# Two more quarters of each MLP's second matrix by seven block products, with the sums kept in DRAM

## The chip, the cores and the metric

The kernel runs on one core of one Trainium2 chip. The metric is the device time of one execution in microseconds (us); lower is better.

## The reference

A trunk of two layers on one sequence of 512 frames of width 1024, all in float32. Layer 0 has a gated linear recurrence (HGRN2), layer 1 a differential attention over keys and values projected once between the layers. Each mixer is followed by an output projection and an MLP, with an RMS norm ahead of and behind each part, and a residual sum:

```python
def squared_relu_mlp(h, w_up, w_down):
    u = jax.nn.relu(h @ w_up)
    return (u * u) @ w_down
...
    for layer in range(DEPTH):
        if layer < N_A:
            ...
            h = h + rms_norm(mix, a_norm_post[a])
        else:
            ...
            h = h + rms_norm(mix, b_norm_post[bi])
        ff = squared_relu_mlp(rms_norm(h, mlp_norm_pre[layer]), mlp_w_up[layer], mlp_w_down[layer])
        h = h + rms_norm(ff, mlp_norm_post[layer])
        if layer == N_A - 1:
            k_sh, v_sh = shared_kv(h, kv_norm, w_kv)
```

The MLP's inner width is 4096; here it is cut into four quarters of 1024. The change is in the two MLPs and in what they share buffers with.

## The kernel before

**Products.** Everything is kept transposed (features on the 128 partitions, frames along a row). A float32 product is made of three products of rounded halves: high by high, high by low, low by high (`mm3`, L114 for each matmul). The activations' halves are `xhi`, `xlo` (the MLP's input) and `uhi`, `ulo` (its inner values). Weights come by SP's DMA into a tile of tag "raw" (four buffers of 512 KB); ACT makes the high half `whi`, DVE the low half `wlo` (eight buffers each).

**Order.** `Plan` writes TensorE's order by hand; the instructions of the other engines stand in the order that the scheduler gave when the kernel was built. An engine takes its instructions, and each queue its transfers, in that fixed order, so a waiting instruction holds all that stands behind it. ACT's and DVE's queues hold splits of weights and evictions of PSUM one behind the other.

**The MLP (`block`).** Quarter 0 of the first matrix is dense (`up`, in two halves of the frames). Quarters 1 to 3 of it go by seven block products (`up_pair`): two row blocks of 128 outputs by two halves of 256 frames, as a 2 x 2 block matrix. One pair has seven products (PSUM names ux, uy, uz) of twelve matmuls of 256 columns, and there are four pairs p to a quarter. `sums_x` makes the sums of x's blocks once. The weights' sums are made per pair: raw_a holds the blocks a11 and a12; raw_s gets the block of row 3 twice by SP, and then the rows 0 and 1 are added to it by a DMA that GpSimd (POOL) issues with accumulate (L465); two sums of DVE (L473, L474) follow, in raw_a's place. raw_d holds the remaining block for two pairs. So two pairs take five raw tiles out of four buffers. The products' results are combined by ACT (p1, p5 and u2: copies out of PSUM, L486) and DVE (L496, L498, L500), then relu (L501, L502, L504), square (L409), uhi (L410), ulo (L411).

After each quarter's first matrix stands that quarter of the second matrix, dense: 192 matmuls of 512 columns (`dn`), whose sums DVE accumulates in the SBUF tile zacc (L538 the first time, L540 later). The last quarter is made by halves of the frames (`dn_h`, `dn_last`), so that the norm behind it (`bounds`) can start with the first half.

So TensorE's order in an MLP is: up, dn quarter 0, four pairs, dn quarter 1, four pairs, dn quarter 2, four pairs, dn quarter 3 by halves.

`params` (the attention's constants and the table bias_dr, written to DRAM by a POOL DMA of 1.25 MB) is spawned as a chain beside layer 0's output projection and MLP.

Of the kernel before, what the change touches and what calls it, by code (L numbers as in the profile page):

```python
# [17 lines left out]
P = 128  # L18
# [70 lines left out]
def trunk_kernel(ctx: ExitStack, tc: tile.TileContext, x_t, w_qf, w_g, w_i, w_ao, w_k, w_q, w_v, w_bo, w_up, w_us, w_dn,  # L89
# [44 lines left out]
    ones1 = cp.tile([P, P], F32, name="ones1")  # L134
    v.memset(ones1, 1.0)
# [25 lines left out]
    def split_w(raw, gain, pr, name):  # L161
# [3 lines left out]
        lo = wp.tile([P, per, ncols], F32R, tag="wlo", name=f"wlo_{name}_{pr}", bufs=8)  # L165
# [14 lines left out]
    def load_w(src, ncols, gain, name):  # L180
        out = []
        for pr in range(ncols // 128):
            out += split_w(fetch_w(src, ncols, pr, name), gain, pr, name)
        return out

# [71 lines left out]
    def bounds(pool, ps_list, zacc, h, gpost, eab, want, name, gpre=None):  # L257
# [92 lines left out]
        if want == "ea":  # L350

            a.activation(ea[:, lo:hi], ms, AF.Square, scale=math.sqrt(EPS), bias=eps15)
        else:
            s = rsqrt_rows((tmp[:, 3, 0], tmp[:, 3, 1]), ms, None)
            a.activation(rb[:, lo:hi], s, AF.Copy, scale=-0.5)
            yield W_RSTD
            pc = smt("ps_rc")
            for i in range(n // P):
                pe.matmul(pc[:, i:i + 1], rb[0:1, lo + i * P:lo + (i + 1) * P], ones1[0:1, 0:1], start=True, stop=True)
            v.tensor_copy(rcol[:, lo // P:hi // P], pc[:, :n // P])  # L360
# [26 lines left out]
    def out_proj(wsrc, gain, name, before_last):  # L387
        wt = [load_w(wsrc[i], 512, gain, f"{name}{i}") for i in range(2)]
        return by_halves(wt, uhi, ulo, name, before_last)

    def block(pool, proj, gpost, name, layer, want):

        gpre = gn[:, G_MPRE[layer]:G_MPRE[layer] + 8]
        zacc = pool.tile([P, 8, S], F32, name=f"zacc{layer}")
# [8 lines left out]
        def split_u(ps, pr, lo, hi, n):  # L403
            r = pool.tile([P, 2, S], F32, tag="r", name=n, bufs=2)[:, :, 0:hi - lo]
            a.activation(r, ps, AF.Relu)
            keep_u(r, pr, lo, hi)

        def keep_u(r, pr, lo, hi):
            a.activation(r, r, AF.Square)  # L409
# [31 lines left out]
        def split_b(raw, name):  # L441

            n = raw.shape[1]
            hi = wp.tile([P, 2, 512], F32R, tag="whi", name=f"whi_{name}", bufs=8)[:, 0:n, :]
            lo = wp.tile([P, 2, 512], F32R, tag="wlo", name=f"wlo_{name}", bufs=8)[:, 0:n, :]
# [4 lines left out]
        a22s = []  # L450

        def up_pair(q, p, ts):

            nm = f"{layer}_{q}_{p}"
# [3 lines left out]
            ws = w_us[layer, q - 1]  # L458
# [7 lines left out]
            if p % 2 == 0:  # L466
                rd = raw("d")
                nc.sync.dma_start(rd, ws[p:p + 2, :, 1, :].rearrange("a p f -> p a f"))
                a22s[:] = split_b(rd, f"d{nm}")
            a11, a12 = split_b(ra, f"a{nm}")  # L470
            a22 = a22s[p % 2]
# [4 lines left out]
            px, py, pz = mmt(f"ux{nm}")[:, 0:256], smt(f"uy{nm}")[:, 0:256], smt(f"uz{nm}")[:, 0:256]  # L476
            r = pool.tile([P, 2, S], F32, tag="r", name=f"r{nm}", bufs=2)
# [6 lines left out]
            def keep(ps, name):  # L484
                t = pool.tile([P, 256], F32, tag="ev", name=f"{name}{nm}", bufs=4)
# [3 lines left out]
            yield from prod(px, a11, xpart(0, 0), True)  # L489
            p1 = keep(px, "p1")  # L490
            yield from prod(pz, s1, ts[0], True)
            p5 = keep(pz, "p5")
            yield from prod(px, s2, ts[2], False)
            u2 = keep(px, "u2")
            yield from prod(py, a12, xpart(1, 0), True)
            v.tensor_tensor(r[:, 0, 0:256], py, p1, op=ALU.add)  # L496
            yield from prod(px, s3, ts[1], False)
            v.tensor_tensor(r[:, 1, 256:512], px, p5, op=ALU.add)  # L498
            yield from prod(pz, s4, xpart(1, 1), False)
            v.tensor_tensor(r[:, 0, 256:512], pz, u2, op=ALU.add)  # L500
            a.activation(r[:, 0, :], r[:, 0, :], AF.Relu)  # L501
            a.activation(r[:, 1, 256:512], r[:, 1, 256:512], AF.Relu, scale=-1.0)  # L502
            yield from prod(px, a22, ts[3], False)
            a.activation(r[:, 1, 0:256], px, AF.Relu, scale=-1.0)  # L504
            keep_u(r, p, 0, S)

        for q in range(4):
            if q == 0:
                wt = [load_w(w_up[layer, i], 512, None, f"up{layer}_{i}") for i in range(2)]
                for h, (lo, hi) in enumerate(halves):  # L510
                    yield until(("x", name, h))
                    for pr in range(4):
                        ps = mmt(f"up{layer}_{h}_{pr}").rearrange("p (j t) -> p j t", j=2)
                        for j in range(2):
                            n = 2 * pr + j
                            for kt in range(8):
                                wmm(ps[:, j, :], wt[n // 4], kt, (n % 4) * P, xhi, xlo, lo, hi, kt == 0, kt == 7)
                                yield 0
                        split_u(ps, pr, lo, hi, f"r{layer}_{h}_{pr}")
                ts = sums_x()  # L520
            else:
                for p in range(4):
                    yield from up_pair(q, p, ts)
            if q < 3:
                for i in range(2):
                    wt = load_w(w_dn[layer, q, i], 512, None, f"dn{layer}_{q}_{i}")
                    pss = [mmt(f"dn{layer}_{q}_{i}_{n4}") for n4 in range(4)]
                    if i == 0:
                        order = [(kt, n4) for kt in range(8) for n4 in range(4)]
                    else:  # L530
                        order = [(kt, n4) for n4 in range(4) for kt in range(8)]
                    for kt, n4 in order:
                        wmm(pss[n4], wt, kt, n4 * P, uhi, ulo, 0, S, kt == 0, kt == 7)
                        if kt == 7:
                            n = 4 * i + n4
                            z = zacc[:, n, :]
                            if q == 0:
                                v.tensor_copy(z, pss[n4])  # L538
                            else:
                                v.tensor_tensor(z, pss[n4], z, op=ALU.add)  # L540
                        yield 0
            else:
                wt = [load_w(w_dn[layer, q, i], 512, None, f"dn{layer}_{q}_{i}") for i in range(2)]
                h = 0
                for r in by_halves(wt, uhi, ulo, f"dn{layer}"):
                    if isinstance(r, list):
                        spawn(bounds(pool, r, zacc, h, G_MPOST[layer], ea, want, f"m{layer}"), 0.3)
                        h += 1
                    else:
                        yield r  # L550
# [532 lines left out]
```

## Time and profile before

| | |
|---|---|
| time, median of 3 runs | 1294.33 us (1294.25 to 1295.51) |
| the profiled execution | 1293.45 us, its span 1291.6 |
| TensorE matmul (PE) | 1256.5 us, 97% |
| VectorE (DVE) | 824.1 us, 64% |
| ScalarE (ACT) | 665.2 us, 52% |
| GpSimd (POOL) | 78.4 us, 6% |
| mean granted TensorE clock | 0.992 |

The profile is of one execution; times in it are from the start of its span. In the chain of waits a row is a stretch of time and the work that ended last in it: start, length, engine, and tile or line. In a timeline a row is one instruction or a run of like ones: start, length, engine, line, operation, out<-in, sizes, and in brackets how long its engine sat idle ahead of it and what ended that. "SPq" and "POOLq" are rows of DMA issues; a DMA's row in the list of issues has its size and the time from issue to landing. q0 is the queue of POOL's transfers, q1 that of SP's.

### The profile page before, as it was taken

To read this page: it belongs to the slowest core of one execution; us is meant where nothing else is said; L and a number is where in the kernel's file an instruction comes from. 1 tells how busy PE (TensorE), PEld (TensorE's weight loads), DVE (VectorE), ACT (ScalarE), POOL (GpSimd) and SP (SyncE) were. 2 spreads that over 40 slices of the span, in tenths; PEclk is the share of its full clock that TensorE was granted. 3 is DMA by queue.
4 is the path that set the end of the run, shared out by engine and by line. 5 is a ranking of instruction groups with operands and counts; after the bars stand their busy time and mean duration, and the time that the engine had idled before them with its cause. 6 is when DMAs were issued, how large, how long until landed. Compare 5 with 4: busy or idle time off the path is not lost.

```text
span 1291.6 us, 21535 instructions
## 1 busy us (share of the span) xinstructions
PE 1256.5 (97%) x8450; PEld 1139.7 (88%) x8450; DVE 824.1 (64%) x1731; ACT 665.2 (52%) x1321; POOL 78.4 (6%) x149
## 2 busy tenths in 40 slices
PE   8999999999997999999998999999999999999996
PEld 7989898999986989989998887889998898988996
DVE  7987777647853554636487978764785463663635
ACT  7553535247732634616454887674773371551732
POOL 0210101010000000000100000001000000000010
PEclk9999999999999999999998999999999999999998
DMA  6322222134355374544614432323336355463521
GB/s 242 110 82 66 66 66 82 50 101 154 108 147 96 101 203 99 172 104 115 212 51 154 139 107 70 103 69 95 129 110 160 94 171 120 115 180 81 167 79 66
DMA packets 53415, 149.89 MB, mean 116 GB/s; under 512 B 6049, under 2 KB 8354, under 8 KB 53314
## 3 DMA queue, kind: packets, MB, share of 16 engines
q1 hardware_dynamic: 44864, 119.82, 29.4%
q0 software_dynamic: 8208, 28.58, 10.1%
q8 instruction: 66, 1.08, 0.3%
q14 instruction: 35, 0.29, 0.1%
q10 hardware_dynamic: 242, 0.13, 0.0%
HBM read 138.80 MB, written 9.70 MB: 115 GB/s over the span
## 4 chain that ended last, share of the span: by engine, by line
PE 53%; ACT 5%; DVE 5%; DMA 4%; issue 1%; DVEq 0%; ACTq 0%; POOLq 0%; SPq 0%
PE dn L114 17%; PE kq L114 6%; PE dn_h L114 5%; PE ux L114 5%; PE up L114 4%; PE v L114 3%; PE bo_h L114 3%; DMA raw_s<-in_w_us_dram 3%; PE uz L114 2%; PE lg L114 2%; PE ao L114 1%; PE uy L114 1%; DVE wlo_s L447 1%; PE pt L119 1%; ACT r L409 1%
## 5 line engine op out<-in xcount | busy, mean ns | idle before, releaser
L114 PE MATMUL dn<-uhi,whi_dn 128*128 128x512 f32 x384 | 152.0, 396 | 0.0
L114 PE MATMUL dn<-ulo,whi_dn 128*128 128x512 f32 x384 | 151.9, 396 | 0.0
L114 PE MATMUL dn<-uhi,wlo_dn 128*128 128x512 f32 x384 | 151.9, 395 | 0.0
L168 DVE TENSOR_TENSOR wlo_dn<-raw_dn,whi_dn 128x1024 fp32r<-128x1024 f32 x64 | 77.5, 1221 | 17.9 <-ACT whi_dn L167 16.8
L446 ACT ACTIVATE whi_a<-raw_a 128x1024 fp32r<-128x1024 f32 x24 | 25.4, 1058 | 122.7 <-PE dn L114 114.1
L114 PEld LDWEIGHTS dn<-uhi,wlo_dn 128*128 128x128 f32 x384 | 72.2, 188 | 17.4
L114 PEld LDWEIGHTS dn<-uhi,whi_dn 128*128 128x128 f32 x384 | 72.2, 188 | 17.3 <-issue 0.2
L114 PEld LDWEIGHTS dn<-ulo,whi_dn 128*128 128x128 f32 x384 | 72.2, 188 | 17.1
L167 ACT ACTIVATE whi_dn<-raw_dn 128x1024 fp32r<-128x1024 f32 x64 | 67.1, 1055 | 17.9 <-PE ux L114 5.5
L114 PE MATMUL up<-xhi,whi_up 128*128 128x256 f32 x256 | 72.7, 284 | 0.0
L114 PE MATMUL up<-xlo,whi_up 128*128 128x256 f32 x256 | 71.9, 281 | 0.0
L114 PE MATMUL up<-xhi,wlo_up 128*128 128x256 f32 x256 | 71.9, 281 | 0.0
L411 DVE TENSOR_TENSOR ulo<-r,uhi 128x1024 fp32r<-128x1024 f32 (+1 forms) x40 | 40.2, 1009 | 47.0 <-ACT uhi L410 47.0
L114 PE MATMUL dn_h<-uhi,whi_dn 128*128 128x256 f32 x240 | 67.8, 282 | 0.0
L114 PE MATMUL dn_h<-ulo,whi_dn 128*128 128x256 f32 x240 | 67.4, 281 | 0.0
L114 PE MATMUL dn_h<-uhi,wlo_dn 128*128 128x256 f32 x240 | 67.4, 281 | 0.0
L540 DVE TENSOR_TENSOR zacc<-dn,zacc 128x512 f32<-128x512 f32 x32 | 22.1, 690 | 57.9 <-PE dn L114 57.8
L114 PE MATMUL qf<-xhi,whi_qf 128*128 128x512 f32 x128 | 53.1, 415 | 1.2 <-ACT xhi L601 0.9
L114 PE MATMUL qf<-xlo,whi_qf 128*128 128x512 f32 x128 | 50.8, 397 | 1.0 <-DVE xlo L602 1.0
L465 POOL DMA_DIRECT2D raw_s<-in_w_us_dram x24 | 20.8, 866 | 494.3 <-DMA raw_s<-in_w_us_dram 334.7
L114 PE MATMUL qf<-xhi,wlo_qf 128*128 128x512 f32 x128 | 50.6, 395 | 0.0
L114 PEld LDWEIGHTS up<-xlo,whi_up 128*128 128x128 f32 x256 | 48.2, 188 | 0.1
(373 smaller groups left out, 4102.3 us busy)
## 6 DMA issues: line engine op xcount, KB each, us to landing
raw_dn<-in_w_dn_dram SPq DMA_DIRECT2D x64, 512.0 KB, 4.4
raw_a<-in_w_us_dram SPq DMA_DIRECT2D x24, 512.0 KB, 4.3
raw_s<-in_w_us_dram SPq DMA_DIRECT2D x48, 256.0 KB, 4.5
raw_s<-in_w_us_dram POOLq DMA_DIRECT2D x24, 512.0 KB, 6.5
raw_up<-in_w_up_dram SPq DMA_DIRECT2D x16, 512.0 KB, 3.9
raw_qf<-in_w_qf_dram SPq DMA_DIRECT2D x15, 512.0 KB, 3.9
raw_d<-in_w_us_dram SPq DMA_DIRECT2D x12, 512.0 KB, 4.4
raw_wi<-in_w_i_dram SPq DMA_DIRECT2D x8, 512.0 KB, 3.8
```

Source lines behind the costliest of these rows:

```text
L114: nc.tensor.matmul(out, lhsT, rhs, **kw)
L119: nc.tensor.transpose(out, in_, identity)
L167: a.activation(hi, raw, AF.Copy)
L168: v.tensor_tensor(lo, raw, hi.bitcast(F32), op=ALU.subtract)
L409: a.activation(r, r, AF.Square)
L411: v.tensor_tensor(ulo[pr][:, :, lo:hi], r, uhi[pr][:, :, lo:hi].bitcast(F32), op=ALU.subtract)
L446: a.activation(hi, raw, AF.Copy)
L447: v.tensor_tensor(lo, raw, hi.bitcast(F32), op=ALU.subtract)
L465: g.dma_start(rs, ws[p, :, 0:2, :], accum_op=ALU.add)
L540: v.tensor_tensor(z, pss[n4], z, op=ALU.add)
```

## The change

Quarters 1 and 2 of the second matrix also go by seven block products (`down_pair`), with the weights in a new input `w_ds` of the same form as `w_us`. `pair` and `blocks_of` are what the up pairs and the down pairs have in common. The blocks of u that a down pair multiplies, and their sums (tu, tv: high and low halves), are made after each up pair by `keep_blocks`. The result of one down pair lies in a tile st and goes to the DRAM tensor zdr by `put_z`, a POOL DMA that adds (the dense quarter 0 writes zdr first: ACT evicts it into st, and `put_z` copies). Ahead of the last quarter the sums come back into zacc by two SP DMAs (L634). The first up pair of the next quarter is computed ahead of the downs of a quarter (`up_pair(q + 1, 0, ts, "rh")`). So each MLP now has twenty pairs in one row between dn quarter 0 and dn quarter 3: u1_0 to u1_3, u2_0, d1_0 to d1_3, u2_1 to u2_3, u3_0, d2_0 to d2_3, u3_1 to u3_3.

For room, whi and wlo have seven buffers, "ev" (p1, p5, u2) three; big tiles share slots (work8, work16, room), and for that one weight tile of each output projection is loaded and split a second time (`again`). `params` starts at other times of the plan, and the matrix ones1 is gone.

```diff
-        hi = wp.tile([P, per, ncols], F32R, tag="whi", name=f"whi_{name}_{pr}", bufs=8)
+            hi = wp.tile([P, per, ncols], F32R, tag="whi", name=f"whi_{name}_{pr}", bufs=7)
...
+        def again(room):
+
+            wt[1][6:] = split_w(fetch_w(wsrc[1], 512, 3, name + "_2"), gain, 3, name + "_2", room)
...
-        zacc = pool.tile([P, 8, S], F32, name=f"zacc{layer}")
+        zacc, room = work("xz")
+        zdr = dr.tile([P, 8, S], F32, name=f"zdr{layer}")
+        again(room)
...
+        def keep_blocks(r, p, tu, tv):
+
+            b = r.rearrange("p j (n t) -> p (j n) t", n=2)
+            t = pool.tile([P, 2, 256], F32, tag="tf", name=f"tf{layer}_{p}", bufs=1)
+
+            def parts(to, src):
+                a.activation(to[:, 0, p], src, AF.Copy)
+                v.tensor_tensor(to[:, 1, p], src, to[:, 0, p].bitcast(F32), op=ALU.subtract)
+
+            v.tensor_tensor(t, b[:, 0:4:3, :], b[:, 1:2, :].to_broadcast([P, 2, 256]), op=ALU.subtract)
+            parts(tu, t)
+            v.scalar_tensor_tensor(t[:, 0, :], t[:, 0, :], -1.0, b[:, 3, :], op0=ALU.mult, op1=ALU.subtract)
+            v.scalar_tensor_tensor(b[:, 1, :], t[:, 0, :], -1.0, b[:, 2, :], op0=ALU.mult, op1=ALU.subtract)
+            keep_u(r, p, 0, S)
+            parts(tv, t[:, 0, :])
...
+        todo = ([(ups[0], p) for p in range(4)] + [(ups[1], 0)] + [(dns[0], m) for m in range(4)] + [(ups[1], p) for p in (1, 2, 3)]
+                + [(ups[2], 0)] + [(dns[1], m) for m in range(4)] + [(ups[2], p) for p in (1, 2, 3)])
...
-            if p % 2 == 0:
+            if not a22s:
+
                 rd = raw("d")
-                nc.sync.dma_start(rd, ws[p:p + 2, :, 1, :].rearrange("a p f -> p a f"))
+                for i in range(2):
+                    w, n = todo.pop(0)
+                    nc.sync.dma_start(rd[:, i, :], w[n, :, 1, :])
...
+        def put_z(n, st, first):
+
+            g.dma_start(zdr[:, n:n + 2, :], st, accum_op=ALU.bypass if first else ALU.add)
+
+        def down_pair(q, m, tu, tv):
+            st = pool.tile([P, 2, S], F32, tag="r", name=f"st{layer}_{q}_{m}", bufs=2)
+
+            def last(n, out, ps, p5):
+                if n == 0:
+                    v.scalar_tensor_tensor(out, ps, -1.0, p5, op0=ALU.mult, op1=ALU.subtract)
+                else:
+                    a.activation(out, ps, AF.Copy, scale=-1.0)
...
+            put_z(2 * m, st, False)
...
+                    if n4 % 2 == 0:
+                        st = pool.tile([P, 2, S], F32, tag="r", name=f"st{layer}_0_{i}_{n4}", bufs=2)
+                    a.activation(st[:, n4 % 2, :], pss[n4], AF.Copy)
+                    if n4 % 2 == 1:
+                        put_z(4 * i + n4 - 1, st, True)
+                yield 0
+        for q in (1, 2):
...
+                if q == 1 or p > 0:
                     yield from up_pair(q, p, ts)
...
+                keep_blocks(made[p], p, tu, tv)
+            yield from up_pair(q + 1, 0, ts, "rh")
+            for m in range(4):
+                yield from down_pair(q, m, tu, tv)
+        keep_u(made[0], 0, 0, S)
+        for p in range(1, 4):
+            yield from up_pair(3, p, ts)
+            keep_u(made[p], p, 0, S)
+        zacc, room = work("z")
+        for lo, hi in halves:
+            nc.sync.dma_start(zacc[:, :, lo:hi], zdr[:, :, lo:hi])
...
-            spawn(params(mp), 60.0)
+            spawn(params(mp), 70.0)
```

In the names below, u1_1_2 is layer 1, quarter 1, pair 2 of the first matrix, d1_1_2 the same of the second; the long numbers tell tiles apart. POOL's queue around layer 1's second and third quarter, before:

```order
L465 DMA raw_s1_1_0_10498<-in_w_us_dram 128x1024
L465 DMA raw_s1_1_1_10627<-in_w_us_dram 128x1024
L465 DMA raw_s1_1_2_10750<-in_w_us_dram 128x1024
L465 DMA raw_s1_1_3_10879<-in_w_us_dram 128x1024
L465 DMA raw_s1_2_0_11258<-in_w_us_dram 128x1024
L465 DMA raw_s1_2_1_11387<-in_w_us_dram 128x1024
```

and after:

```order
L502 DMA raw_sd1_1_0_11729<-in_w_ds_dram 128x1024
L502 DMA raw_sd1_1_1_11848<-in_w_ds_dram 128x1024
L502 DMA raw_sd1_1_2_11974<-in_w_ds_dram 128x1024
L568 DMA zdr1_9952<-st1_1_0_11726 128x1024
L502 DMA raw_sd1_1_3_12093<-in_w_ds_dram 128x1024
L568 DMA zdr1_9952<-st1_1_1_11845 128x1024
L502 DMA raw_su1_2_1_12231<-in_w_us_dram 128x1024
L568 DMA zdr1_9952<-st1_1_2_11971 128x1024
L502 DMA raw_su1_2_2_12362<-in_w_us_dram 128x1024
L568 DMA zdr1_9952<-st1_1_3_12090 128x1024
L502 DMA raw_su1_2_3_12500<-in_w_us_dram 128x1024
```

From the third down pair on, each adding DMA for the weights stands behind the adding DMA that carries a pair's result three pairs earlier to zdr.

ACT's queue where the splits for a pair meet the evictions of the pairs ahead (L486 and L532 are the copies p1, p5, u2 out of PSUM), before:

```order
L446 ACTIVATE whi_a_1_3_10883<-raw_a_1_3_10877 128x1024
L446 ACTIVATE whi_s_1_3_10887<-raw_s_1_3_10879 128x1024
L502 ACTIVATE r_1_1_10648<-r_1_1_10648 128x256
L501 ACTIVATE r_1_1_10648<-r_1_1_10648 128x512
L504 ACTIVATE r_1_1_10648<-ux_1_1_10645 128x256
L409 ACTIVATE r_1_1_10648<-r_1_1_10648 128x1024
L486 ACTIVATE p_1_2_10790<-ux_1_2_10774 128x256
```

and after, among the down pairs of layer 1:

```order
L482 ACTIVATE whi_td1_1_1_11869<-raw_ad1_1_1_11846 128x1024
L482 ACTIVATE whi_ad1_1_2_11978<-raw_ad1_1_2_11972 128x1024
L482 ACTIVATE whi_sd1_1_2_11982<-raw_sd1_1_2_11974 128x1024
L577 ACTIVATE st1_1_0_11726<-xd1_1_0_11747 128x256
L532 ACTIVATE p1d1_1_1_11888<-xd1_1_1_11873 128x256
L482 ACTIVATE whi_td1_1_2_11988<-raw_ad1_1_2_11972 128x1024
L532 ACTIVATE p5d1_1_1_11902<-zd1_1_1_11875 128x256
L532 ACTIVATE u2d1_1_1_11916<-xd1_1_1_11873 128x256
```

In both, whi_s of the pair two ahead stands before the last eviction of a pair and before p1 of the next; the eviction it stands before is now the one that zdr's DMA waits for.

SP's queue behind a run of up pairs in layer 1, before:

```order
L464 DMA raw_s_1_3_10879<-in_w_us_dram 128x512 x2
L158 DMA raw_dn_1_0_0_11000<-in_w_dn_dram 128x1024
L158 DMA raw_dn_1_0_1_11006<-in_w_dn_dram 128x1024
L158 DMA raw_dn_1_0_2_11012<-in_w_dn_dram 128x1024
L158 DMA raw_dn_1_0_3_11018<-in_w_dn_dram 128x1024
```

and after:

```order
L501 DMA raw_su_1_3_11470<-in_w_us_dram 128x512 x2
L497 DMA raw_au_2_0_11599<-in_w_us_dram 128x2x512
L501 DMA raw_su_2_0_11601<-in_w_us_dram 128x512 x2
L508 DMA raw_du_2_0_11605<-in_w_us_dram 128x512
L508 DMA raw_du_2_0_11605<-in_w_ds_dram 128x512
L497 DMA raw_ad_1_0_11727<-in_w_ds_dram 128x2x512
L501 DMA raw_sd_1_0_11729<-in_w_ds_dram 128x512 x2
```

Eight tiles of a dense quarter followed the pairs; now the tiles of the next pairs follow at once.

More of the change, by code (lines that the diff above doesn't have):

```diff
@@ L385, in by_halves, with out_proj, block, work @@
             yield views
[L387 to L391, printed above, removed]
-        gpre = gn[:, G_MPRE[layer]:G_MPRE[layer] + 8]
-        zacc = pool.tile([P, 8, S], F32, name=f"zacc{layer}")
+    def out_proj(pool, wsrc, gain, name, before_last):
+        wt = load_whole(wsrc, gain, name, new_room(pool))
+        def again(room):
+            wt[1][6:] = split_w(fetch_w(wsrc[1], 512, 3, name + "_2"), gain, 3, name + "_2", room)
+        return by_halves(wt, uhi, ulo, name, before_last), again
+    def block(pool, proj, again, gpost, name, layer, want):
+        gpre = gn[:, G_MPRE[layer]:G_MPRE[layer] + 8]
+        def work(name):
+            t = pool.tile([P, 2, 2, 512], F32R, tag="work8", name=f"{name}w{layer}", bufs=1)
+            return pool.tile([P, 8, S], F32, tag="work16", name=f"{name}{layer}", bufs=1), [t[:, 0], t[:, 1]]
+        zacc, room = work("xz")
+        zdr = dr.tile([P, 8, S], F32, name=f"zdr{layer}")
+        again(room)
         h = 0
@@ new lines, in block @@
+        made = {}
+        wt = load_whole(w_up[layer], None, f"up{layer}_", room)
+        for h, (lo, hi) in enumerate(halves):
+            yield until(("x", name, h))
+            for pr in range(4):
+                ps = mmt(f"up{layer}_{h}_{pr}").rearrange("p (j t) -> p j t", j=2)
+                for j in range(2):
+                    n = 2 * pr + j
+                    for kt in range(8):
+                        wmm(ps[:, j, :], wt[n // 4], kt, (n % 4) * P, xhi, xlo, lo, hi, kt == 0, kt == 7)
+                        yield 0
+                split_u(ps, pr, lo, hi, f"r{layer}_{h}_{pr}")
@@ new lines, in block @@
+        keep_u(made[0], 0, 0, S)
[5 more added lines that the diff above has]
+            nc.sync.dma_start(zacc[:, :, lo:hi], zdr[:, :, lo:hi])
+        wt = load_whole(w_dn[layer, 1], None, f"dn{layer}_3_", room)
+        h = 0
+        for r in by_halves(wt, uhi, ulo, f"dn{layer}"):
+            if isinstance(r, list):
+                spawn(bounds(pool, r, zacc, h, G_MPOST[layer], ea, want, f"m{layer}"), 0.3)
+                h += 1
+            else:
+                yield r
@@ L996, in main @@
         with tc.tile_pool(name="mlp1", bufs=1, reuse_waits="tile") as mp:
-            yield from block(mp, chain([r], proj), G_BPOST, "bo", 1, "out")
+            yield from block(mp, chain([r], proj), again, G_BPOST, "bo", 1, "out")
             yield until(("out", 0), ("out", 1))
```

176 lines of the change are left out of this document (87 added, 89 removed).

## Prediction

> **What bounds the kernel now.** I read the engine totals first, then the chain of waits in order of time through the second layer's MLP, then windows over the four quarters in which the weights come as blocks, then the timelines of SP, POOL, ACT and DVE over one lap of the weight buffers.
>
> ```profile
> PE 1256.5 (97%) x8450; PEld 1139.7 (88%) x8450; DVE 824.1 (64%) x1731; ACT 665.2 (52%) x1321; POOL 78.4 (6%) x149
> 627.67 27.69 PE dn_h L114 x234
> 974.23 44.80 PE dn L114 x192
> 1019.04 1.42 PE ux L114 x12
> 1020.46 1.42 PE uz L114 x12
> 1030.25 7.13 DMA raw_s<-in_w_us_dram
> 1060.44 44.80 PE dn L114 x192
> 1146.93 44.80 PE dn L114 x192
> 1233.20 27.69 PE dn_h L114 x234
> ```
>
> The first row gives busy time, share and instructions of each engine; the others are steps of the chain: start, length, what ran. TensorE sets the end nearly everywhere: a dense down quarter is 192 matmuls of 512 columns in 44.80 us, and one block product is 12 matmuls in 1.42. Between two dense quarters stand four pairs of seven products. But in the first pairs of each such run the chain leaves TensorE for an adding DMA into raw_s: the ring of four raw tiles is nearly as slow as TensorE even there.
>
> ```profile
> 404.00:454.80 50.80, 42.97 (x338) 42.16 (x337) 26.20 (x33) 26.87 (x41) 0.86 (x1) 0.93 0.52 122
> 1019.00:1060.40 41.40, 40.62 (x338) 40.20 (x337) 28.21 (x36) 29.34 (x44) 0.86 (x1) 1.00 0.53 156
> 1105.20:1146.90 41.70, 40.64 (x338) 40.21 (x337) 28.24 (x36) 29.37 (x44) 0.86 (x1) 1.00 0.53 156
> 398.65 0.68 POOL L662 DMA_DIRECT2D bias_dr<-tb  x1 [10.58 <-DVE tb L661]
> 403.98 0.28 PE L114 MATMUL ux<-xhi,whi_a 128*128 128x256 f32 x1
> 416.40 0.80 PE L114 MATMUL ux<-t,whi_s 128*128 128x256 f32 x2 [6.55 <-ACT u L486]
> 415.02 1.06 ACT L446 ACTIVATE whi_d<-raw_d 128x1024 fp32r<-128x1024 f32 x1 [7.61 <-DMA raw_d<-in_w_us_dram]
> ```
>
> The windows (length; busy time of PE, weight load, DVE, ACT, POOL; granted clock; DMA share; GB/s) show four pairs in 41.4 to 41.7 us, so **10.35 a pair**, against 7 x 1.42 = 10.0 of products. Layer 0's first run takes 50.8: TensorE waits 6.55 us for a late raw_d (through ACT's queue), and the granted clock falls to 0.93. That is 9.4 us beyond 41.4, 6.55 of it the wait. The stretch that changes runs from the end of the first dense down quarter to the start of dn_h: 627.67 - 403.98 = **223.7 us in layer 0** and 1233.20 - 1019.04 = **214.2 in layer 1**.
>
> **The change part by part.** Removed per layer: two dense down quarters, 2 x 44.80. Put in their place: eight down pairs of seven products. So each layer gets 20 pairs in one row. At 10.35 each that is 207.0, and the change would gain 223.7 - 207.0 = 16.7 and 214.2 - 207.0 = 7.2, 23.9 together. The question is whether 20 pairs in a row can run at 10.35. Before, a run of four pairs starts with tiles fetched and split during the dense quarter ahead, whose 44.8 us let the ring catch up; now only the first pairs of the row have that. So the price is the lap time of the ring. One lap (two pairs) in layer 1:
>
> ```profile
> 1017.60 1.22 DVE L447 TENSOR_TENSOR wlo_s<-raw_s,whi_s 128x1024 fp32r<-128x1024 f32 x1
> 1018.85 0.38 SPq L468 DMA_DIRECT2D raw_d<-in_w_us_dram  x1
> 1022.71 1.06 ACT L446 ACTIVATE whi_d<-raw_d 128x1024 fp32r<-128x1024 f32 x1 [0.41 <-DMA raw_d<-in_w_us_dram]
> 1023.80 1.22 DVE L447 TENSOR_TENSOR wlo_d<-raw_d,whi_d 128x1024 fp32r<-128x1024 f32 x1 [1.95 <-ACT whi_d L446]
> 1025.05 0.82 SPq L464 DMA_DIRECT2D raw_s<-in_w_us_dram  x2
> 1030.25 0.86 POOL L465 DMA_DIRECT2D raw_s<-in_w_us_dram  x1 [24.97 <-DVE raw_a L474]
> 1036.96 0.42 DVE L498 TENSOR_TENSOR r<-ux,p 128x256 f32<-128x256 f32 x1
> 1037.45 1.06 ACT L446 ACTIVATE whi_s<-raw_s 128x1024 fp32r<-128x1024 f32 x1 [1.67 <-DMA raw_s<-in_w_us_dram]
> 1038.55 1.23 DVE L447 TENSOR_TENSOR wlo_s<-raw_s,whi_s 128x1024 fp32r<-128x1024 f32 x1 [1.17 <-ACT whi_s L446]
> 1040.02 0.68 DVE L473 TENSOR_TENSOR raw_a<-raw_a,raw_s 128x512 f32<-128x512 f32 x1
> 1040.14 0.63 ACT L501 ACTIVATE r<-r 128x512 f32<-128x512 f32 x1 [1.32 <-DVE r L500]
> 1042.04 0.37 ACT L486 ACTIVATE p<-ux 128x256 f32<-128x256 f32 x1
> 1042.46 0.51 PE L114 MATMUL ux<-t,whi_t 128*128 128x256 f32 x2 [0.50 <-ACT p L486]
> ```
>
> Every step starts when the one ahead ends: wlo_s frees the slot (1018.82), raw_d loads, is split, frees the slot for raw_s at 1025.05; the two copies, then the adding DMA, 12.4 us to whi_s; and at 1040.70 the last reader of raw_s is through. The lap is 1040.70 - 1018.82 = **21.9 us for two pairs, 10.95 a pair**, and behind whi_s on ACT the eviction p holds TensorE for 0.50 us. TensorE's two pairs want 20.7 at most. Now the terms.
>
> First three pairs of the row: their tiles are made beside the dense quarter, as before: 10.35 each.
>
> Six up pairs whose u is also summed for the downs (keep_blocks): DVE does L442 ahead of the sum L513 (L473 before) that frees the slot: 0.68 by the row of L473, same shape; and wlo_d now stands behind L555, which waits for the fifth product, and whi_d for the fourth product's release of one of seven buffers (it waited for its DMA alone): bounds 0 to 0.4. 21.9 + 0.7 + 0.1 = 22.7 a lap, **11.35 a pair**. The added work itself (DVE 0.69 + 0.69 + 3 x 0.42 = 2.6, ACT 0.63 + 0.37 = 1.0 a pair, from the rows of such shapes) has room: 28.21 / 4 + 2.6 = 9.7 of DVE and 29.34 / 4 + 1.0 = 8.3 of ACT.
>
> Eight down pairs: the ring without these sums, 10.95. But put_z, a second adding DMA, stands on POOL between the weights' adds: raw_s of pair p+3 behind zdr of pair p, and whi_s(p+2) on ACT ahead of the eviction into st that zdr(p) waits for. So one turn is whi_s, then st, zdr's issue, the raw_s add to landing, whi_s: 1.06 + 0.37 + 0.86 + 7.1 = 9.4 if zdr's bytes cost the add nothing.
>
> ```profile
> 909.34 14.90 PE bo_h L114 x126
> q0 software_dynamic: 144, 0.52, 36.7%
> raw_s<-in_w_us_dram POOLq DMA_DIRECT2D x1, 512.0 KB, 7.1
> raw_s<-in_w_us_dram POOLq DMA_DIRECT2D x24, 512.0 KB, 6.5
> raw_dn<-in_w_dn_dram SPq DMA_DIRECT2D x64, 512.0 KB, 4.4
> L540 DVE TENSOR_TENSOR zacc<-dn,zacc 128x512 f32<-128x512 f32 x32 | 22.1, 690 | 57.9 <-PE dn L114 57.8
> ```
>
> In the 8 us from 1030 one add took 36.7% of all engines, 2.9 us. If zdr's transfer of as many bytes is served first, the turn is 9.4 + 2.9 = 12.3. No row shows an adding DMA into DRAM; below, the ring's 10.95 remains, above 12.3. Since the queues' transfers overlap (two are open in these 8 us), I take a value nearer to the ring: **11.35**.
>
> A rule of the Trainium skill bears on this: its page DMA: Bandwidth & Descriptors, section Anatomy of one DMA, fits a GpSimd transfer as 2.0 us plus its bytes by 436 GB/s, so an estimate of 3.2 us for these 512 KB. The trace has 6.5 to 7.1 and so does not agree for an adding one.
>
> Last three up pairs: nothing is summed beside them and the ring runs out: halfway between 10.35 and 11.35, 10.8.
>
> Sum per layer: 3 x 10.35 + 6 x 11.35 + 8 x 11.35 + 3 x 10.8 = 222.4. Layer 0: 222.4 - 223.7 = -1.3 (the 6.55 us stall goes: the bias_dr transfer, issued at 398.65 and so beside the late raw_d, is now issued into the dense quarter, with 44.8 us over it). Layer 1: 222.4 - 214.2 = +8.2.
>
> Costed at nothing: quarter 0's sums evicted by ACT instead of DVE, and four put_z, since no accumulation waits (if the cover goes, 4 x 0.86 of POOL before the third pair's add); DVE's zacc accumulations go (x32 at 0.69), but they lay beside matmuls; seven split buffers in place of eight in the dense parts; again(), one tile loaded and split twice per layer, 4.4 + 1.06 + 1.22 = 6.7 us with out_proj's matmuls (the row bo_h and those around it) over it (bounds 0 and 6.7 each); the reload of the sums by two SP transfers ahead of six raw_dn tiles: it can start when the last put_z has landed, three pairs (over 31 us) ahead of dn_h.
>
> Together +6.9 on the profiled execution's 1293.45 (span 1291.6 plus 1.85), 1300.3; the median of the runs, 1294.33, lies 0.9 above it, so **1301**.
>
> **The rivals.** A: the ring keeps TensorE's pace. For it: 10.35 holds for four pairs, the median add lands in 6.5 and not 7.1, and the raw_dn prefetches beside the lap go away. raw_s from issue to whi_s must fall from 12.4 to 11.2 (lap 20.7). Against: the lap row by row, and the 0.50 us wait within the third pair already. Time: 1294.3 - 23.9 = 1270. By the fit of the Trainium skill's page DMA: Bandwidth & Descriptors, given above, the add would land about 3.9 us earlier and this would be the case. Between: the waits bind partly, 10.5 to 11.0 a pair over the 14 middle pairs, so 28 x 0.35 to 0.85 less than the forecast: 1277 to 1291.
>
> B (forecast): 11.0 to 11.9 a pair, 1291 to 1317.
>
> C: put_z is served in full before the weights' add, as a second 7.1 in the turn: 16.5 a down pair, 16 x 5.15 = 82 more, 1383; it decides from where an add lands later than some 8.7 us after its issue (turn over 11.0). For it: one queue, q0, carries both. Against: 2.9 us of engine time each. A smaller form: waits of some us in every pair lower the clock, as 6.55 did above (0.50 left it at 1.00).
>
> On that the Trainium skill's page TensorE: Matmul & The Clock Gate, Part 1, puts the fall to half rate after an idle window of about 3.4 us; the trace agrees as far as 0.50 and 6.55 lie on its two sides.
>
> D: the stall of layer 0 stays in another place, beside the seven-buffer ring: +9.4, 1310, within B's range.
>
> **How the numbers follow.** A 0.14, between 0.20, B with D 0.50, C (over 1317) 0.16. No change that can be told is within 0.2%, 2.6 us: 1291.7 to 1296.9, some 0.09, all from B's low end. Faster 0.34, same 0.09, slower 0.57. The range leaves out half of A below and two thirds of C above: 1271 to 1332; for B alone 1291 to 1317.
>
> **What would show it.** Right: in the windows from the first dense quarter's end to dn_h 222 us a layer; the chain there made of raw_s, zdr and whi_s steps in nearly every second pair; TensorE's waits 0.5 to 2 us each, named p or u on ACT; raw_s to whi_s still over 12 us. Wrong: 10.35 a pair throughout (the ring faster than its lap row) or adds that land after 10 us and more in the down pairs (C). Layer 0 should no longer wait 6.55 us anywhere in its first pairs.

## The result

| | before | after |
|---|---|---|
| time, median of 4 runs | 1294.29 us (1294.05 to 1295.51) | 1376.53 us (1374.81 to 1377.76) |
| ratio | | 1.0632, 95% interval 1.0614 to 1.0651 |
| profiled execution, its span | 1293.45, 1291.6 | 1377.76, 1376.0 |
| mean granted TensorE clock | 0.992 | 0.965 |

The change costs 82 us; 1301 was forecast. Engine totals and the last chain rows after (the chain is followed back to 1228 us; start, length, what):

```profile
PE 1265.0 (92%) x9026; PEld 1177.9 (86%) x9026; DVE 896.7 (65%) x1868; ACT 735.3 (53%) x1459; POOL 110.2 (8%) x189
1256.56 9.94 DMA raw_su<-in_w_us_dram
1269.92 10.04 DMA raw_du<-in_w_us_dram
1317.18 27.68 PE dn_h L114 x234
```

TensorE's busy time grows by 8.5 us (1256.5 to 1265.0), although eight down pairs of 10.0 us each are less work than the 89.6 us a layer that they replace: the products run at a slower clock. The rest of the 84 us is waiting. The windows over the stretch that changes, from the end of the first dense down quarter to dn_h, layer 0 and layer 1, first of before, then of after (columns as in the prediction):

```profile
404.00:627.60 223.60, 214.08 (x1394) 194.76 (x1393) 120.50 (x144) 107.89 (x152) 12.07 (x17) 0.98 0.54 142
1019.00:1233.20 214.20, 211.54 (x1395) 192.82 (x1394) 120.25 (x144) 108.18 (x152) 12.05 (x17) 1.00 0.53 144
```

```profile
404.40:668.70 264.30, 217.64 (x1682) 213.63 (x1681) 160.23 (x220) 137.78 (x213) 27.40 (x36) 0.92 0.71 170
1058.30:1317.00 258.70, 216.54 (x1681) 212.47 (x1680) 159.87 (x220) 137.29 (x212) 27.52 (x35) 0.92 0.71 171
```

437.8 us became 523.0: +85.2, the whole loss. The clock column falls to 0.92. What TensorE waited for after (us in total, times, longest):

```profile
PE xd L114 <- DVE st L575: 57.4, 8, 7.8
PE xu L114 <- ACT p1u L532: 10.7, 6, 4.3
PE xu L114 <- DVE r L555: 10.5, 6, 5.9
PE xd L114 <- ACT p1d L532: 7.3, 7, 1.7
```

Eight waits of some 7 us, one in every second down pair, make two thirds of the row's 88 us of waits (the four rows and 2.3 us more behind ACT's u2d). The length of each pair of the row, from the first matmul of one pair to that of the next in TensorE's timeline (us; u1_0 to u1_3, u2_0 | d1_0 to d1_3 | u2_1 to u2_3, u3_0 | d2_0 to d2_3 | u3_1 to u3_3):

```
layer 0  10.0 16.1 10.6 11.2 12.6 | 11.8 20.4 11.4 18.7 | 10.1 18.6 11.0 10.0 | 11.6 18.5 11.1 18.7 | 11.5 10.0 10.2
layer 1  11.0 10.1 10.5 12.4 12.5 | 12.0 19.7 11.1 19.4 | 11.2 14.8 10.2 10.0 | 11.4 20.3 11.4 19.2 | 11.5 10.0 10.0
```

One of the long pairs, d2_1 of layer 1, in the timelines, from the transfer that starts it to the product that waits:

```profile
1237.77 0.88 POOL L568 DMA_DIRECT2D zdr<-st  x1 [8.86 <-ACT p1d L532]
1238.35 1.18 POOL L502 DMA_DIRECT2D raw_sd<-in_w_ds_dram  x1
1239.13 0.33 SPq L508 DMA_DIRECT2D raw_dd<-in_w_ds_dram  x1
1239.50 0.75 SPq L508 DMA_DIRECT2D raw_dd<-in_w_us_dram  x1
1249.40 1.06 ACT L482 ACTIVATE whi_dd<-raw_dd 128x1024 fp32r<-128x1024 f32 x1 [7.97 <-DMA raw_dd<-in_w_us_dram]
1250.49 1.23 DVE L483 TENSOR_TENSOR wlo_dd<-raw_dd,whi_dd 128x1024 fp32r<-128x1024 f32 x1 [8.01 <-ACT whi_dd L482]
1251.63 0.42 DVE L575 SCALAR_TENSOR_TENSOR st<-xd,p5d 128x256 f32<-128x256 f32 x1
1252.10 0.58 PE L114 MATMUL xd<-uhi,whi_dd 128*128 128x256 f32 x1 [7.52 <-DVE st L575]
```

Two adding transfers go out within 0.6 us, zdr's and the weights'. SP asks for raw_d's two halves right behind them (1239.13 and 1239.50), and the second lands 10 us later instead of 3.9. ACT waits 7.97 us for it, DVE's wlo_d waits for ACT, and L575, ready long before, stands behind wlo_d. L575 reads the PSUM tile that the seventh product is to be written to, so TensorE waits for a tile of weights that only later pairs need (raw_dd here holds d2_3's and u3_1's). The add for raw_sd, issued 0.6 us behind zdr's transfer, lands 10.8 us after its issue, 0.2 us ahead of raw_d; its split, whi_sd, stands two places behind whi_dd in ACT's queue.

The long u2_2 has the same pattern with no zdr transfer beside it: in layer 0 raw_d, issued at 541.25 beside the weights' add alone, is split at 549.52, and L555, the up pairs' counterpart of L575, stands behind wlo_d; TensorE waits 5.9 us.

### The profile page after: what moved, and what is told of

Same layout as the page of the kernel before. It is cut to its first block, busy times and chain, and to the rows that moved or that the text cites. A ratio compares the mean times of both kernels' runs of the same rounds, so it can differ in the third digit from the quotient of the medians.

```text
span 1376.0 us, 23353 instructions
## 1 busy us (share of the span) xinstructions
PE 1265.0 (92%) x9026; PEld 1177.9 (86%) x9026; DVE 896.7 (65%) x1868; ACT 735.3 (53%) x1459; POOL 110.2 (8%) x189
## 5 line engine op out<-in xcount | busy, mean ns | idle before, releaser
L114 PE MATMUL xd<-uhi,whi_dd 128*128 128x256 f32 x48 | 19.3, 401 | 57.4 <-DVE st L575 57.4
L483 DVE TENSOR_TENSOR wlo_tu<-raw_au,whi_tu 128x1024 fp32r<-128x1024 f32 x24 | 29.3, 1222 | 42.7 <-ACT whi_tu L482 42.7
L114 PE MATMUL dn<-uhi,whi_dn 128*128 128x512 f32 x128 | 50.8, 397 | 0.2 <-ACT r L425 0.2
L114 PE MATMUL dn<-ulo,whi_dn 128*128 128x512 f32 x128 | 50.6, 396 | 0.0
L114 PE MATMUL dn<-uhi,wlo_dn 128*128 128x512 f32 x128 | 50.6, 395 | 0.0
L483 DVE TENSOR_TENSOR wlo_du<-raw_du,whi_du 128x1024 fp32r<-128x1024 f32 x12 | 14.7, 1225 | 52.9 <-ACT whi_du L482 52.8
L114 PE MATMUL xu<-t,whi_tu 128*128 128x256 f32 x192 | 37.5, 293 | 10.9 <-ACT p1u L532 10.7
L169 DVE TENSOR_TENSOR wlo_dn<-raw_dn,whi_dn 128x1024 fp32r<-128x1024 f32 x30 | 36.2, 1222 | 13.6 <-ACT whi_dn L168 13.1
L114 PEld LDWEIGHTS gl<-q,k 128*126 128x126 f32 (+5 forms) x384 | 40.7, 173 | 4.1 <-issue 1.6
L114 PE MATMUL gl<-q,k 128*126 128x64 f32 (+5 forms) x384 | 42.0, 254 | 0.5 <-DVE sc L792 0.5
```

Source lines behind the costliest of these rows:

```text
L114: nc.tensor.matmul(out, lhsT, rhs, **kw)
L169: v.tensor_tensor(lo, raw, hi.bitcast(F32), op=ALU.subtract)
L483: v.tensor_tensor(lo, raw, hi.bitcast(F32), op=ALU.subtract)
```

## The experiments

The theory, T: in the long row of pairs raw_d's load meets adding transfers, runs two to three times as long where it meets two, and the order of ACT's and DVE's queues turns that into waits of TensorE. Its rivals: R1, it is the adding to DRAM that is dear, not a transfer as such; R2, POOL's order (an add for weights held behind a zdr transfer that waits for st); R3, the ring itself is too slow (seven buffers, four raw tiles, the sums of u); R4, the amount of traffic, wherever it is put.

**1. No zdr transfers in quarters 1 and 2.**

```diff
-            put_z(2 * m, st, False)
```

> The changed kernel, with the adding transfers of the down pairs' results to zdr left out in quarters 1 and 2 (the output then lacks these two quarters of each MLP); everything else stands. T (zdr's transfer and the weights' add, both in POOL's queue, are in flight while SP loads raw_d, whose load takes 10 us in place of 3.9, and the queues of ACT and DVE hold TensorE behind it): the eight waits at DVE L575 of some 7 us fall under 1 us, down pairs at 11.5 us or less each, time 1298 to 1315. R3 (the ring is too slow by itself: seven split buffers, four raw tiles, no dense quarter to catch up in, the sums of u on DVE): the waits stay, 1350 or more. R2 (POOL's order alone: the weights' add stands behind a zdr transfer that waits for st) also expects 1298 to 1315 here.

Measured: 1339.75 us (1335.35 to 1342.79), ratio 1.0357 (1.0338 to 1.0376). So 37 of the 82 us are zdr's, and 45 are not. Every recorded range missed: T and R2 had 1298 to 1315, R3 1350 or more, and T's 11.5 us or less for a down pair came for six of the sixteen (10.0 to 17.0 in all). The waits, and one window per layer over the row:

```profile
PE xd L114 <- DVE st L575: 19.2, 7, 4.3
PE xu L114 <- ACT p1u L532: 15.5, 8, 4.5
PE xu L114 <- DVE r L555: 13.5, 5, 5.7
404.20:645.70 241.50, 212.39 (x1682) 208.60 (x1681) 160.09 (x220) 138.65 (x213) 20.39 (x28) 0.95 0.67 168
1035.90:1274.40 238.50, 210.78 (x1681) 206.54 (x1680) 160.23 (x220) 137.79 (x212) 19.80 (x26) 0.97 0.66 168
```

The row is still 480 us, with waits of 4 to 6 us, and u2_2 is no shorter without zdr's transfers (19.1 and 17.2 us).

**2. The same transfers as plain copies, by POOL and then by ACT.**

```diff
-            put_z(2 * m, st, False)
+            g.dma_start(zdr[:, 2 * m:2 * m + 2, :], st)
```

> The changed kernel, with the transfers to zdr in quarters 1 and 2 as plain copies in place of adding ones, in the same places of POOL's queue (each overwrites the sums, so the output lacks what it should have added to). T by traffic: a copy of the same 512 KB still takes engine time beside raw_d, but without reading the old sums: raw_d 6 to 8 us, time 1320 to 1355. R1 (it is the adding that is dear): 1298 to 1315, as without any. R2 (POOL's order): 1365 or more, unchanged.

```diff
-            put_z(2 * m, st, False)
+            a.dma_start(zdr[:, 2 * m:2 * m + 2, :], st)
```

> As the kernel with plain copies, but the copies are issued by ACT and not by POOL, so that nothing but the weights' adds is left in POOL's queue in the row of pairs. R2 (POOL's order and its one queue): 1298 to 1315. T by traffic, whatever the queue: near the kernel with plain copies, within 15 us of it. [...]

Measured: 1343.84 us (1337.96 to 1350.01), ratio 1.0381 (1.0336 to 1.0427), and 1340.39 us (1336.17 to 1343.79), ratio 1.0353 (1.0325 to 1.038). Neither can be told from the kernel without the transfers, or from the other. So of zdr's 37 us nearly all is that the transfer adds. That is R1 for this part, by its words "as without any"; its range, 1298 to 1315, missed with experiment 1. POOL's order is not the price: R2 expected 1365 or more with POOL's copies and 1298 to 1315 with ACT's. T's range for the copies, 1320 to 1355, holds, and so in part does its reason: beside a copy and the weights' add started together, raw_d's load still takes 7.8 to 8.3 us in layer 1, and the waits at L575 are 30.2 us against experiment 1's 19.2; but the other waits are shorter, and the row's waits come to 57 us against 56. How much longer an adding transfer takes is seen in the list of issues (KB each, median us to landing): adding in the changed kernel, then copying by POOL, then by ACT.

```profile
zdr<-st POOLq DMA_DIRECT2D x24, 512.0 KB, 5.5
```

```profile
zdr<-st POOLq DMA_DIRECT2D x24, 512.0 KB, 3.8
```

```profile
zdr<-st ACTq DMA_DIRECT2D x16, 512.0 KB, 3.3
```

(Eight of the 24 are quarter 0's plain ones in the first two.)

**3. No adding transfers for the weights; DVE makes the sums.** One plain load brings rows 1 and 3 of a pair's weights, a22 is split from it, and two additions on DVE make s1 and s3; put_z stays.

```diff
-            for i in range(2):
-                nc.sync.dma_start(rs[:, i, :], ws[p, :, 3, :])
-            g.dma_start(rs, ws[p, :, 0:2, :], accum_op=ALU.add)
+            nc.sync.dma_start(rs, ws[p, :, 1:4:2, :])
...
+            a.activation(a22[0], rs[:, 0, :], AF.Copy)
+            v.tensor_tensor(a22[1], rs[:, 0, :], a22[0].bitcast(F32), op=ALU.subtract)
+            v.tensor_tensor(rs[:, 0, :], rs[:, 0, :], rs[:, 1, :], op=ALU.add)
+            v.tensor_tensor(rs[:, 1, :], rs[:, 1, :], ra[:, 0, :], op=ALU.add)
```

> The changed kernel with put_z as it is, but no adding DMA for the weights: rows 1 and 3 of a pair's weights come in one plain SP load into raw_s, a22 is split from it, and DVE makes the sums s1 and s3 (two more additions of 128x512, 0.69 us each, a pair; two raw tiles a pair and not two and a half, 1 MB loaded a pair and not 1.75 MB moved and 0.5 MB read again). T: without the 12 us chain of copies and add in the ring, and with one adding transfer in flight and not two, a load that takes 6 us is early enough: no wait over 1.5 us, 20 pairs at 10.2 to 11 us each, time 1275 to 1300. R3 (buffers and DVE are what is short): over 1330, since DVE gets 1.4 us a pair more and the buffers are as many.

Measured: 1293.96 us (1291.65 to 1296.67), ratio 0.9996 (0.9985 to 1.0006), within T's range; R3's bound of 1330 falls. T's smaller signs missed: three kinds of waits in the row pass 1.5 us (r L553 up to 2.2, p1d 2.1, p1u 1.8), and the pairs take 10.0 to 13.8 us, 10.9 on average.

```profile
408.60:627.30 218.70, 204.86 (x1681) 202.44 (x1682) 177.94 (x262) 140.14 (x222) 12.29 (x18) 0.99 0.48 138
1017.00:1233.70 216.70, 204.96 (x1681) 202.37 (x1680) 180.37 (x265) 139.39 (x221) 11.75 (x17) 0.99 0.48 139
PE xu L114 <- DVE r L553: 16.3, 14, 2.2
```

The row takes 435.4 us, hardly under the 437.8 of before. DVE is now busy for 178 to 180 us of some 217, and it is what TensorE waits for most in the up pairs.

**4. Only the weights' add left out, nothing else touched.** This keeps the raw tiles, the buffers and DVE's work as in the changed kernel.

```diff
-            g.dma_start(rs, ws[p, :, 0:2, :], accum_op=ALU.add)
```

> The changed kernel with the adding transfers of the weights left out (raw_s holds row 3 twice, so the block products are of wrong sums), put_z and everything else as it is: the same raw tiles, the same two and a half of them a pair, the same buffers. T (the serial chain raw_d, two copies, add, together with the meeting of raw_d and the adds): the lap loses the 8 us of the add, raw_d meets one adding transfer and not two, waits under 1.5 us: 1280 to 1305. R3 (four raw buffers at two and a half tiles a pair, seven split buffers): over 1325.

Measured: 1295.05 us (1291.41 to 1298.63), ratio 1.0002 (0.9987 to 1.0017). T had 1280 to 1305, R3 over 1325. So neither four raw buffers at two and a half tiles a pair, nor seven split buffers, nor the sums of u cost much: R3 is out. Its pairs u1_1 to u2_0 take 10.0 to 10.4 us. Most of what TensorE still waits for in the row are the eight waits at L575 (now L574), shorter. The first row below is their sum, the second one of them; the others are the windows over the two rows of pairs and one right behind that wait:

```profile
PE xd L114 <- DVE st L574: 16.1, 8, 2.3
1090.58 0.49 PE L114 MATMUL xd<-uhi,whi_dd 128*128 128x256 f32 x1 [2.29 <-DVE st L574]
407.60:627.90 220.30, 209.60 (x1681) 208.21 (x1682) 156.93 (x217) 139.06 (x213) 12.33 (x18) 0.96 0.57 158
1017.60:1236.20 218.60, 208.01 (x1681) 206.37 (x1680) 159.28 (x220) 138.49 (x212) 11.77 (x17) 0.97 0.59 159
1090.70:1094.10 3.40, 3.40 (x17) 3.40 (x18) 3.37 (x5) 0.51 (x2) 0.00 (x0) 0.50 0.57 154
```

Seven of the eight waits, 1.75 to 2.29 us long, have such 3.4 us at a clock of 0.50 within 1 us of their end; so even these short waits cost more than their own length. What this run cannot tell apart: leaving the add out takes it away from beside raw_d, and also takes the add's own time out of each pair's chain of loads and splits.

**5. The zdr transfers of the even down pairs moved.** All transfers stay; a one-column operation on POOL holds an even pair's zdr transfer until the next pair's fourth product.

```diff
+            if held:
+                n, st = held.pop()
+                z0 = pool.tile([P, 1], F32, tag="z0", name=f"z0{nm}", bufs=1)
+                g.tensor_scalar(z0, out[:, 0, 0:1], 0.0, None, op0=ALU.mult)
+                g.tensor_tensor(st[:, 0, 0:1], st[:, 0, 0:1], z0, op=ALU.add)
+                put_z(n, st, False)
...
-            put_z(2 * m, st, False)
+            if m % 2 == 0:
+                held.append((2 * m, st))
+            else:
+                put_z(2 * m, st, False)
```

> The changed kernel, all its transfers kept (adding ones to zdr too), but the zdr transfer of each even down pair is held, by a one-column POOL operation that reads the next pair's first result, until the fourth product of the next pair, and so no longer starts within 1.5 us of raw_d's load. T (it is the meeting of raw_d's load with two adding transfers that costs): raw_d to whi_d 5 to 7 us in the down pairs and not 9 to 10.5, time 1335 to 1360, near the kernel without the transfers. R4 (the amount: half a megabyte added per pair loads the engines wherever it is put): 1368 or more.

Measured: 1351.46 us (1345.8 to 1355.45), ratio 1.0435 (1.0409 to 1.0462): 25 us less than the changed kernel, with the same transfers and the same adds; T had 1335 to 1360, R4 1368 or more. R4 falls for that part: the place costs, not the amount. Raw_d's way from SP's issue to whi_d, read row by row in the timelines of SP, POOL and ACT, in layer 1's row (nine loads; for before layers 0 and 1, the load issued beside bias_dr left out), by what POOL had issued since shortly before the load:

| in flight beside raw_d | before | after | zdr left out | zdr later | weights' add left out |
|---|---|---|---|---|---|
| nothing | 3.8 to 4.1 | | | | 3.9 to 4.5 |
| three loads of SP, issued in the 4 us ahead | 5.3 to 7.7 | | | | |
| the weights' add | | 4.3 to 6.3 | 4.3 to 7.9 | 4.5 to 6.1 | |
| zdr's transfer | | | | | 6.1 to 6.6 |
| both, started together | | 9.3 to 10.5 | | | |
| both, zdr 4 us later | | | | 5.8 to 7.3 | |

(Left out of the table are the first loads of the row, 5.4 to 6.3, beside a plain zdr copy of quarter 0.) One adding transfer makes the load 1 to 2 us longer on average, two at once 6. The weights' adds themselves stretch as well: the sixteen of the changed kernel's two rows that follow a zdr transfer (from the fourth down pair of each run on, not from the third as said ahead of the prediction) land 7.9 to 10.8 us after their issue, 9.5 on average, the others in 5.7 to 8.7.

**6. Does zdr cost anything without the weights' adds?** Experiment 3 without the zdr transfers of quarters 1 and 2.

> The changed kernel with s1 and s3 summed by DVE and the zdr transfers of quarters 1 and 2 left out (the output lacks them). T: without the weights' adds in the ring the zdr transfers are covered, so leaving them out gives 0 to 6 us against the same kernel with them (1294): 1288 to 1295. If zdr's traffic costs whatever else is in flight: 1275 or less.

Measured: 1283.03 us (1282.75 to 1283.63), ratio 0.9914 (0.9899 to 0.9929). So zdr's transfers cost 11 us even there; T had 0 to 6, the other side 19 or more, and neither holds. The lengths of the pairs show where: the last three up pairs take 68.0 us in both layers together with the transfers and 60.1 without, d1_2 takes 26.2 and 22.0, and all others together 1 us less with them.

**7. DVE relieved by GpSimd.** In experiment 3, first s1 and s3 on GpSimd (`v.tensor_tensor(rs...)` becomes `g.tensor_tensor(rs...)`), then, with these on DVE, the first difference of u's blocks (L442).

> The changed kernel without adding DMAs for the weights, with s1 and s3 summed by GpSimd and not by DVE (DVE gets 1.4 us a pair back). If what is left over 10 us a pair there is DVE's load (its waits before the seventh product, 16 us over both layers): 1278 to 1290. If GpSimd takes over 2.5 us for an addition of 128x512, or stands behind a zdr transfer that waits for st: 1296 or more.

> The changed kernel with s1 and s3 summed by DVE, and the first difference of u's blocks (L442, 0.69 us, one a pair in eight pairs a layer) moved to GpSimd. DVE's load theory: 3 to 8 us faster than with it on DVE, 1285 to 1291. If a hop over GpSimd costs as much as it frees: 1292 to 1297.

Measured: 1319.17 us (1316.18 to 1321.77), ratio 1.0193 (1.0177 to 1.0209), and 1304.35 us (1300.1 to 1309.45), ratio 1.0077 (1.0056 to 1.0098). Both are slower than experiment 3, and the ranges recorded for a gain (1278 to 1290, 1285 to 1291) missed. GpSimd's addition of 128x512 takes twice DVE's 0.69 us, and DVE's own next sum runs longer than in experiment 3 (0.68 us there), as the groups of the first of the two show:

```profile
L509 POOL TENSOR_TENSOR raw_su<-raw_su,raw_au 128x512 f32<-128x512 f32 x24 | 37.0, 1544 | 1.8
L511 DVE TENSOR_TENSOR raw_au<-raw_au,raw_su 128x512 f32<-128x512 f32 x24 | 27.2, 1132 | 22.8 <-POOL raw_su L509 22.7
```

DVE waits 22.7 us for GpSimd there. The slower outcome, 1296 or more, was right, but neither of its conditions came: the additions take 1.3 to 1.6 us on average and not 2.5, and in layer 1's row POOL idles ahead of them until DVE's wlo_d, never behind a zdr transfer. In the second run the first difference takes 1.84 us on GpSimd, and both of its ranges missed.

**8. The same cure in the kernel before.** Its weights' sums by DVE, as in experiment 3; then also `spawn(params(mp), 70.0)` and `yield 8.0` as in the changed kernel.

> The kernel before, its weights' sums s1 and s3 by DVE from one plain load (as in the variant of the changed kernel), no adding DMA for weights. If the adding DMA in the ring is a price in the kernel before too: the four-pair runs go from 41.5 to 40.5 us and layer 0's stall of 6.6 us goes, since no raw_d is loaded beside bias_dr alone: 1278 to 1290. If not (the dense quarters cover it, or DVE with 1.4 us a pair more takes its place): 1292 to 1297.

> The kernel before with s1 and s3 summed by DVE, and the attention's constants made at the times of the changed kernel (spawned at 70 with a wait of 8, not at 60 with 40), so that bias_dr's transfer is issued beside the dense quarter and not beside layer 0's first pairs. If bias_dr is what holds TensorE 5 us there: the first pair of layer 0's row falls from 16.7 to about 10.7 us and the time to 1280 to 1284. If not: 1286 to 1290.

Measured: 1288.34 us (1287.11 to 1288.96), ratio 0.995 (0.9937 to 0.9963), and 1281.66 us (1281.1 to 1282.76), ratio 0.9904 (0.9889 to 0.9918). The first lies within the 1278 to 1290 of the adding DMA's price, but both signs named for it missed: layer 1's runs of four went from 41.5 to 41.0 us on average and not to 40.5, and layer 0's stall did not go. Its first pair took 16.7 us, with a wait of 5.0 at L499: raw_s's load, issued at 406.87 with bias_dr's transfer in flight, was split at 416.11. With the constants made earlier (bias_dr issued at 374.9 and not at 398.5) that pair takes 10.4, as expected. This is the fastest of the versions that leave nothing out, 12.6 us under the kernel before, with the second matrix dense in all quarters:

```profile
PE 1254.3 (98%) x8450; PEld 1137.6 (89%) x8450; DVE 853.2 (67%) x1791; ACT 666.2 (52%) x1333; POOL 57.6 (5%) x125
```

## Why the prediction was wrong

Its frame held: the loss lies between dn and dn_h alone (+85.2 of +84.3 profiled), layer by layer 264.3 and 258.7 against the 222.4 of its sum.

- **First three pairs**, 31.05: 31.6 in layer 1, 36.7 in layer 0. The 6.55 us stall was said to go with bias_dr. It came back as 16.1 us in u1_1 (waits up to 4.3), beside the two zdr copies of quarter 0 and the weights' add: raw_d was issued at 407.41 and split at 416.24. Without the weights' add (experiment 4) u1_1 takes 10.0. Rival D was right on that, for another transfer.
- **Six up pairs**, 68.1: 73.5 and 71.1. The excess is in u2_2 (18.6 and 14.8), by a raw_d late beside the weights' add: it stays without zdr's transfers (19.1 and 17.2) and is 13.9 and 11.5 without the add; the others average 11.1. The seven buffers and the sums of u were costed right or too high: experiment 4 ran the six pairs in 65.4 and 62.5.
- **Eight down pairs**, 90.8: 122.2 and 124.5. This is the step that failed, 65 of the 78 us that the row came out over its forecast. It has three errors. First, the lap of 21.9 us was read where raw_d loaded alone (3.9 us), right behind a dense quarter. In the long row raw_d's load falls beside a weights' add, and takes 4.3 to 7.9 us there. Before's trace has no load of raw_d that meets an add over more than its last 1.8 us, so it could not show that meeting; but it does show that the 3.9 us do not hold beside other traffic. For the first pairs of the later runs of four, raw_d goes out behind three loads of SP and takes 5.3 to 7.7 us, in the dense quarter, where nothing waits for it; the prediction does not use these loads. Experiment 1's laps in layer 1, from raw_d's issue to the next one's, are 22.2 to 26.8 us, mean 24.1, without any zdr transfer in the down pairs. Second, put_z was priced as bytes ahead of the weights' add on POOL's path, as a chain beside the ring; but its transfer starts within 1.5 us of raw_d's load and stretches that, in the ring: laps of 29.5 to 30.4. Third, every wait was counted once. The sum has no term for the clock, though the stall of layer 0 before had cost 2.9 us beyond its 6.55: the 40 pairs at 10.0 are 400 us, TensorE's waits in the row are 88 (the four rows above and 2.3 at u2d), and the remaining 35 us are products at a granted clock of 0.92. The prediction also put the fall of the clock at about 3.4 us of idling; experiment 4's 1.75 to 2.29 us were enough, so that dividing line does not hold here. One of the loads that the prediction does not use, in before's timelines:

```profile
539.70 0.56 SPq L460 DMA_DIRECT2D raw_a<-in_w_us_dram  x1
541.16 0.81 SPq L464 DMA_DIRECT2D raw_s<-in_w_us_dram  x2
542.69 0.38 SPq L468 DMA_DIRECT2D raw_d<-in_w_us_dram  x1
548.53 0.86 POOL L465 DMA_DIRECT2D raw_s<-in_w_us_dram  x1 [36.92 <-DMA raw_s<-in_w_us_dram]
550.36 1.06 ACT L446 ACTIVATE whi_d<-raw_d 128x1024 fp32r<-128x1024 f32 x1 [4.97 <-DMA raw_d<-in_w_us_dram]
```

- **Last three**, 32.4: 31.7 and 31.5. Right.
- **Costed at nothing**: outside the row the profiled executions differ by 0.9 us, so evictions, again(), the reload of the sums and the seven buffers in dense parts were hidden as said, or offset each other.
- **Rival C** gave 1383 and is near the time, but its mechanism is not the measured one. It had the weights' add served after zdr's, some 14 us to landing; none in the row took more than 10.8. A part of it is there: the adds behind a zdr transfer took 9.5 us on average, over the 8.7 from which it was to decide. But the waits follow raw_d, a load in SP's queue that it does not name. Its smaller form, that waits of some us lower the clock, came true.
- **Rival A** (1270) needs the adds to go faster; without any adds for weights and without zdr, 1283 was reached, with TensorE's waits in the row mostly at DVE's L553 (11.4 us). The fit of the Trainium skill's page DMA: Bandwidth & Descriptors, section Anatomy of one DMA, gives 3.2 us for 512 KB, as an estimate; POOL's plain copies, at a median of 3.8 us to landing, come near it, and the adding ones at 5.5 to 8.5 do not.

What stays open: why two adding transfers at once cost three times what one costs; how much of the loss is raw_d's stretch and how much the weights' adds' own length, since no run shortens raw_d alone and the two land together in the long pairs; and by what way zdr costs the last up pairs 7.9 us in experiment 6 (all of its 11 us lie in the row, 435.4 against 424.2). That the order of ACT's and DVE's queues carries the wait is read from the timelines; no run changed that order.

## What to carry to other kernels

A lap time read once holds only for what was in flight beside that lap: before a short run of stages is made long, read the same load in all its laps, and keep apart those with other transfers in flight. A transfer that is hidden by its own path can still be dear through a load in another queue that it meets, above all an adding one; here it was cheaper to spend 1.4 us a pair of a DVE that was busy for 61% of the row than to let the DMA add. And a late tile can cost what stands behind its split in ACT's and DVE's queues, before it costs what it feeds.

## What the runs showed of the hardware

- Adding transfers of 512 KB from SBUF into DRAM landed in 5.5 us (median with eight plain ones), plain copies in 3.8 by POOL (the same) and 3.3 by ACT; raw_d's 512 KB reached whi_d in 3.8 to 4.5 us with nothing of POOL's beside it (5.3 to 7.7 right behind three loads of SP), 4.3 to 7.9 beside one adding transfer, 9.3 to 10.5 beside two that started together.
- Moving half of the same adding transfers by some 6 us was worth 25 us of 1376.
- Waits of 7 us in every second down pair left the granted clock of the row at 0.92; eight waits of 1.75 to 2.29 us and one of 2.5 (experiment 4) at 0.96 and 0.97, and seven of the eight had 3.4 us at 0.50 within 1 us of their end; waits of up to 2.2 us (experiment 3) left it at 0.99.
- GpSimd's 128x512 additions took 1.31 to 1.56 us on average, and DVE's addition behind them 1.02 to 1.13 instead of 0.68.
